# The first layer's input projection in another order, with new on-chip places for its branch

## The chip, the cores and the metric

One core of a Trainium2 chip runs the whole program. The metric is the device time of one execution in microseconds (us). Five engines work beside each other, each through its own queue in order: TensorE (PE, with its weight loads PEld), VectorE (DVE), ScalarE (ACT), GpSimd (POOL) and SyncE (SP), which here issues the DMA transfers.

## The reference

Two layers of a diffusion backbone on 1152 columns of width 1024: 1024 latent tokens (conditioned by `c`) and 128 context tokens (conditioned by `c_ctx`). Layer 0 mixes with a bidirectional recurrence and a pooling branch, layer 1 with attention; each has a squared-ReLU MLP behind. What the change touches is the mixer of layer 0:

```python
hp = modulate(x, p['g_mix'], shift, scale)          # rms_norm(x)*(1+scale)+shift
z = h @ p['w_in']                                   # 1024 -> 1536
xr, gate, xpool = jnp.split(z, [D_RNN, 2 * D_RNN], axis=-1)   # 512 each
xc = dwconv_centred(xr, p['conv_w'], p['conv_b'])   # 4 taps along the sequence
r = sigmoid(xc @ w_a + b_a); i = sigmoid(xc @ w_i + b_i)      # both directions
a = exp(8 r log_sigmoid(lam)); u = sqrt(1 - a*a) * (i * xc)
h_t = a_t h_{t-1} + u_t                             # forward and backward scan
y_rnn = (hf + hb) * gelu(gate)
y_pool = ((window mean - xpool) @ w_pool) * s_pool  # windows 2, 4, 8, 16
out = concat([y_rnn, y_pool]) @ p['w_out']
```

The states of the recurrence at the ends of the context are an output too.

## The kernel before

Features lie on the 128 partitions, the sequence along the row. `w_in` is cut into 12 units of 128 output features: 0 to 3 recurrent channels, 4 to 7 gate channels, 8 to 11 pooling groups with windows 2, 4, 8 and 16. The sequence is cut into three chunks of 384 columns (chunk 2 holds 256 latent and 128 context columns). `project(u, hs, c)` computes one unit for one chunk in one PSUM bank: 24 matmuls, since every fp32 operand is split into a high and a low fp32r part and three of their products are summed (`mm3`, lines 166 to 168; `split`, lines 162 and 163: ACT copies the high part, DVE or POOL subtracts for the low part). There are 8 banks.

In the beginning `mod_steps` (line 200) multiplies the conditioning by `w_mod`, for shift and scale of the first norm. `first_norm` squares a chunk (ACT), sums the squares (DVE and POOL by turns), gets the root through two small matmuls (`Norm.stat`, lines 280 and 289) and multiplies (line 383); `modulate` with `inplace` scales and shifts (line 304) and splits. `first_units` then projects units 11, 10 and 9 (u3) as chunks become ready. Units 8, 0, 1, ..., 7 follow in the loop over `order`; behind each chunk stands `hook(w, c)`, which carries the other work of the branch:

- `windows(g, pb)`: the doubling sums of a pooling group (line 556, POOL and DVE by turns), its edges (POOL), the difference (line 563), its split into `xh` and `xl`; in a second step the 9 pooling matmuls, and the store of the result to device memory (lines 573 and 574).
- `conv(m, xr)` (lines 484 and 487, DVE), `gates(m, xc)` (split of `xc` into the same single pair `xh`, `xl`; 36 matmuls; 12 sigmoids, line 507) and `lru(m, xc, z)` (lines 518 to 539: tanh, exp, square root on ACT, products on DVE and POOL, four scans on DVE, the sum of both directions). The four gate results and four temporaries come from a ring of 10 buffers.
- `mod_bg(2)` behind chunks 1 and 2: two steps each of `mod_steps` for the later modulations, each step one weight load and two matmuls, each ninth step a transpose (line 207).

Gates and recurrences stand at units 2 to 5. The GELU and the last product (`rnn_out`, lines 544 and 546) wait until the last square root was issued. Then `out_proj` (first matmul: `ps_b<-mix_yh`) reads the pooled channels back from device memory.

PE's order is the program's; a scheduler sets the others, but for SP's transfers of the beginning. Behind the beginning all loads of weights and for `mod_steps` share three `w_raw` buffers.

Of the kernel before, what the change touches and what calls it, by code (L numbers as in the profile page):

```python
# [77 lines left out]
def emit(tc, A, O):  # L78
# [216 lines left out]
    def modulate(norm, x, c, hs, l, ffn, lo_eng=(po, ve), inplace=False, spare=None):  # L295
# [3 lines left out]
        for k in range(KT):  # L299
            xn = x[c][:, k, :]  # L300
            sh = lambda g: mod[l][:, sh0 + k, g:g + 1]
            if inplace:
                for a, b, g in groups(c, norm.ch):
                    ve.tensor_scalar(xn[:, a:b], xn[:, a:b], scl[:, k, g:g + 1], sh(g), op0=OP.mult, op1=OP.add)
                split(hh[:, k, :], hl[:, k, :], xn, eng=lo_eng[k % len(lo_eng)])
                continue
# [145 lines left out]
    pbs = {}  # L452
    for g in (3, 2, 1):
        pbs[g] = gslot()
        pads(pbs[g], 8)
# [54 lines left out]

    hst = {}

    def lru(m, xc, z):
# [75 lines left out]
    pw = parts(load(A["w_pool"], 512), sl, "wg", 1)  # L589
    wnd = {g: windows(g, pbs[g]) for g in (3, 2, 1)}  # L590
    next(wnd[3])
    ys, xr, xcs, gl_ = {}, {}, {}, {}

    def gate_products(m):
        return lru(m, xcs[m], next(gl_[m]))

    def hook(w, c):

        nonlocal last
# [2 lines left out]
        if w == 8 and c == 2:
            wnd[0] = windows(0, pbs[0])
        at = {(8, 1): 3, (0, 0): 2, (0, 2): 1, (1, 1): 0}.get((w, c))
        if at is not None:
            next(wnd[at])
            if at:
                next(wnd[at - 1])
# [976 lines left out]
```

## Time and profile before

| | us |
|---|---|
| median of 3 runs (lowest, highest) | 2928.2 (2923.76, 2932.3) |
| the profiled execution | 2933.02 |
| its span | 2931.0 |
| PE, DVE, ACT, POOL busy in the span | 2781.7, 1896.3, 1354.9, 1155.2 |

The profile is of one execution, and its times count from the start of its span. A row of the windows shows: from and to, length, busy time of PE, PEld, DVE, ACT and POOL (with counts), PE's granted clock as a share of 2.4 GHz, the DMA engines' busy share, and GB/s. A timeline row shows start and duration of instructions of one line; the time in brackets is how long the engine sat idle before and what released it. Ends of matmuls are modelled, so their starts are read.

### The profile page before, as it was taken

Reading aid. Unit: us, or ns where it says so; the run is one execution under the profiler, and the core shown is the slowest. Engines: PE = TensorE matmul, PEld = TensorE weight load, DVE = VectorE, ACT = ScalarE, POOL = GpSimd, SP = SyncE. Lnnn points to the kernel's source line nnn. Section 1 sums busy time; section 2 is a strip of 40 time slices with the busy share of each in tenths; the row PEclk is TensorE's granted clock in tenths of the full one; section 3 lists DMA queues with packets and bytes.
Section 4 is the critical chain, followed back from the end, with each engine's and each line's share of the span. In section 5 each row is a group of like instructions: output and inputs, shape, how many; then the busy total and the mean of one; then the engine's idle time right before and its main releaser. Section 6 shows DMA issues by size and latency. Waiting matters only on the chain.

```text
span 2931.0 us, 51557 instructions
## 1 busy us (share of the span) xinstructions
PE 2781.7 (95%) x19896; PEld 2685.8 (92%) x19896; DVE 1896.3 (65%) x3534; ACT 1354.9 (46%) x3143; POOL 1155.2 (39%) x968
## 2 busy tenths in 40 slices
PE   5897799999999999898999999998999999999997
PEld 3886698999999999898999999988999999999997
DVE  5559677666555788965777777776841112368887
ACT  3356343222335233455777777774432223433335
POOL 3434111112138878313323233321111112688853
PEclk8999899999999999999999999999999999999998
DMA  5233514666564554420000000024244444455452
GB/s 228 87 124 97 182 44 160 211 211 206 207 224 164 197 188 157 148 70 21 21 14 22 13 15 23 23 63 134 77 169 158 164 153 158 156 194 194 157 163 89
DMA packets 144941, 372.78 MB, mean 127 GB/s; under 512 B 15944, under 2 KB 49080, under 8 KB 143288
## 3 DMA queue, kind: packets, MB, share of 16 engines
q1 hardware_dynamic: 144696, 369.50, 37.2%
q8 instruction: 156, 2.56, 0.4%
q14 instruction: 89, 0.73, 0.1%
HBM read 260.68 MB, written 108.75 MB: 126 GB/s over the span
## 4 chain that ended last, share of the span: by engine, by line
PE 77%; DVE 12%; ACT 4%; issue 3%; DMA 2%; POOL 2%; SPq 0%; DVEq 0%; ACTq 0%; POOLq 0%
PE ps_b L166 19%; PE ps_b L167 19%; PE ps_b L168 19%; PE pS_t L1129 3%; PE pS_o L1147 3%; PE pS_s L166 3%; PE pS_s L168 2%; PE pS_s L167 2%; ACT aw_p L1122 1%; PE pS_g L166 1%; PE pS_g L168 1%; PE pS_g L167 1%; DVE x_t L352 1%; DVE acc_t L827 1%; ACT aw_ph L1133 1%
## 5 line engine op out<-in xcount | busy, mean ns | idle before, releaser
L765 POOL TENSOR_TENSOR fu_r<-fu_r 128x576 f32<-128x576 f32 x128 | 160.4, 1253 | 669.9 <-ACT fu_ah L764 640.7
L167 PE MATMUL ps_b<-ht_t,wl_hlh 128*128 128x288 f32 (+1 forms) x1312 | 404.4, 308 | 13.8 <-DVE ht_t L163 9.2
L166 PE MATMUL ps_b<-ht_t,wl_hlh 128*128 128x288 f32 (+1 forms) x1312 | 407.4, 311 | 6.4 <-ACT ht_t L162 5.0
L168 PE MATMUL ps_b<-ht_t,wl_hll 128*128 128x288 f32 (+1 forms) x1312 | 402.0, 306 | 0.0
L766 DVE TENSOR_TENSOR fu_ah<-fu_r,fu_ah 128x576 fp32r<-128x576 f32 (+1 forms) x128 | 89.1, 696 | 356.1 <-POOL fu_r L765 356.1
L759 ACT ACTIVATE fu_r<-ps_b 128x288 f32<-128x288 f32 x256 | 104.2, 407 | 432.8 <-PE ps_b L168 427.1
L882 DVE TENSOR_TENSOR acc_t<-ps_b,acc_t 128x288 f32<-128x288 f32 x656 | 269.8, 448 | 51.0 <-PE ps_b L168 49.3
L166 PEld LDWEIGHTS ps_b<-ht_t,wl_hlh 128*128 128x128 f32 x1312 | 249.6, 190 | 21.1 <-issue 6.7
L167 PEld LDWEIGHTS ps_b<-ht_t,wl_hlh 128*128 128x128 f32 x1312 | 250.3, 191 | 17.0 <-DVE ht_t L163 10.5
L162 ACT ACTIVATE wl_hlh<-w_raw 128x1024 fp32r<-128x1024 f32 (+1 forms) x161 | 137.7, 863 | 268.4 <-PE ps_b L167 205.0
L1137 DVE TENSOR_TENSOR aw_pl<-pS_t,aw_ph 128x384 fp32r<-128x384 f32 (+1 forms) x400 | 200.5, 541 | 84.7 <-ACT aw_ph L1133 79.1
L168 PEld LDWEIGHTS ps_b<-ht_t,wl_hll 128*128 128x128 f32 x1312 | 250.7, 191 | 0.0
L166 PE MATMUL ps_b<-fq_at,wl_hlh 128*128 128x288 f32 x800 | 238.0, 298 | 1.6 <-DVE acc_t L882 1.1
L168 PE MATMUL ps_b<-fq_at,wl_hll 128*128 128x288 f32 x800 | 235.4, 294 | 0.0
L167 PE MATMUL ps_b<-fq_at,wl_hlh 128*128 128x288 f32 x800 | 234.8, 293 | 0.0
L1122 ACT ACTIVATE aw_p<-pS_s,aw_nb 128x384 f32<-128x384 f32 (+1 forms) x400 | 225.1, 580 | 17.9 <-DVE aw_nb L1116 17.0
L1112 DVE TENSOR_REDUCE aw_mx<-pS_s 128x1 f32<-128x384 f32 (+1 forms) x400 | 203.7, 539 | 34.9 <-PE pS_s L168 33.8
L1133 ACT ACTIVATE aw_ph<-pS_t 128x384 fp32r<-128x384 f32 (+1 forms) x400 | 174.1, 487 | 86.4 <-PE pS_t L1129 85.7
L163 DVE TENSOR_TENSOR wl_hll<-w_raw,wl_hlh 128x1024 fp32r<-128x1024 f32 (+1 forms) x109 | 139.4, 1279 | 99.9 <-ACT wl_hlh L162 98.7
L696 POOL TENSOR_TENSOR fb_b<-fb_b 128x576 f32<-128x576 f32 x112 | 176.6, 1588 | 25.5 <-DMA fb_b<-dram_t 21.6
L166 PE MATMUL ps_b<-fq_at,fw_hlh 128*128 128x288 f32 x576 | 172.0, 299 | 4.6 <-DVE acc_t L882 3.3
L167 PE MATMUL ps_b<-fq_at,fw_hlh 128*128 128x288 f32 x576 | 170.0, 295 | 0.0
(394 smaller groups left out, 8902.1 us busy)
## 6 DMA issues: line engine op xcount, KB each, us to landing
fq_at<-dram_t SPq DMA_DIRECT2D x76, 576.0 KB, 3.9
dram_t<-fu_ah SPq DMA_DIRECT2D x72, 576.0 KB, 2.9
w_raw<-in_ffn SPq DMA_DIRECT2D x64, 512.0 KB, 3.8
dram_t<-fu_r SPq DMA_DIRECT2D x112, 288.0 KB, 2.1
fb_b<-dram_t SPq DMA_DIRECT2D x28, 1152.0 KB
fq_at<-in_w_mod SPq DMA_DIRECT2D x128, 192.0 KB, 4.1
w_raw<-in_l_ffn_w SPq DMA_DIRECT2D x40, 512.0 KB, 4.8
w_raw<-in_w_mod SPq DMA_DIRECT2D x32, 512.0 KB, 4.2
```

The source lines that it names most:

```text
L162: act(hi, src, AF.Copy)
L163: eng.tensor_tensor(lo, src, hi.bitcast(F32), op=OP.subtract)
L166: mm(out, wh, hh, start=start, stop=False)
L167: mm(out, wh, hl, start=False, stop=False)
L168: mm(out, wl, hh, start=False, stop=stop)
L696: po.tensor_tensor(a[:, :, o, :], a[:, :, p, :], a[:, :, q, :], op=op)
L765: po.tensor_tensor(r, r, r, op=OP.mult)
L882: ve.tensor_tensor(to, b, to, op=OP.add)
L1112: ve.tensor_reduce(self.mx[:, i:i + 1], self.sc[i][0], axis=AX.X, op=OP.max)
L1122: act(self.pt[i][:, :w], v, AF.Exp, bias=self.nb, accum_out=lsum[:, self.h, self.blk, i:i + 1])
L1133: act(hi[g][:, :self.nks[g], j * P:(j + 1) * P], self.tp[g], AF.Copy)
L1137: ve.tensor_tensor(lo[g][s_], self.tp[g], hi[g][s_].bitcast(F32), op=OP.subtract)
```

## The change

Units 0, 1 and 2 are projected at first, then 3, 11, 10, 4, 9, 5, 8, 6 and 7. Each recurrence starts as soon as its channels are there; pooling groups and gate channels lie between. GELU and last product stand behind the third chunk of each gate unit. The result of a recurrence is written over its input slot `xr[m]`. The ring has 8 buffers, convolution slots are 3, three `p` slots hold pooling and gate channels, and the pooling weights are loaded group by group. `mod_bg` gets one step behind chunks 0 and 1, two behind chunk 2. The first norm now multiplies scale and root in one pass, the shift is added by ACT (high part) and DVE (low part), as the later norms do it. All splits of `xh` and `xl` and all window sums go to DVE.

```diff
 def first_norm(c):
-            nm.square(c, xin[c][:, k, :], eng=(ve, po)[k % 2])
+            nm.square(c, xin[c][:, k, :], eng=ve)
         yield from nm.stat(c)
-            ve.tensor_tensor(xin[c][:, k, :], xin[c][:, k, :], nm.rs[c], op=OP.mult)
+                ve.scalar_tensor_tensor(xv[:, a:b], xv[:, a:b], sc_mix[0][:, k, g:g + 1], nm.rs[c][:, a:b],
+                                        op0=OP.mult, op1=OP.mult)
+    def shifted(c):
...
+                act(hs[c][0][:, k, a:b], xv[:, a:b], AF.Identity, bias=sh)
+                ve.scalar_tensor_tensor(hs[c][1][:, k, a:b], xv[:, a:b], sh, hs[c][0][:, k, a:b].bitcast(F32),
+                                        op0=OP.add, op1=OP.subtract)
...
-    first_units((1, 2), (1, 1), (2, 3), (2, 2), (2, 1))
+    first_units((1, 1), (1, 2), (2, 0))
-    ring = lambda: sr.t([P, RW], tag="r", bufs=10)[:, :TL]
-    cslot = lambda: sl.t([P, PADW], tag="c", bufs=4)
+    ring = lambda: sr.t([P, TL], tag="r", bufs=8)
+    cslot = lambda: sl.t([P, PADW], tag="c", bufs=3)
+    pslot = lambda: sl.t([P, PADW], tag="p", bufs=3)
 def gates / windows
-        split(xh, xl, xc, eng=po)
+        split(xh, xl, xc)
-            (po, ve)[i % 2].tensor_tensor(nx[:, :n], cur[:, :n], cur[:, k:k + n], op=OP.add)
+            ve.tensor_tensor(nx[:, :n], cur[:, :n], cur[:, k:k + n], op=OP.add)
-        split(dh, dl, d, eng=po)
+        split(dh, dl, d)
+        pw = parts(load(A["w_pool"][:, g * P:(g + 1) * P], P), sl, "pw", 1)
...
+    def recurrence(m):
+        z = next(gl_[m])
+        if m in (1, 2):
+            next(wnd[4 - m])
+        lru(m, xcs[m], z)
+        if m < 3:
+            xcs[m + 1] = conv(m + 1, xr[m + 1])
+
+    HOOKS = {(3, 0): [(recurrence, 0), (before_gates, 1)], (10, 0): [(recurrence, 1)],
+             (4, 0): [(next, 3), (before_gates, 2)], (9, 0): [(recurrence, 2)],
+             (5, 0): [(next, 2), (before_gates, 3)], (8, 0): [(recurrence, 3), (next, 1)],
+             (6, 0): [(next, 1), (next, 0)], (7, 0): [(next, 0)]}
 def hook(w, c):
-        if c:
-            mod_bg(2)
...
+        mod_bg(1 + (c == 2))
+        for f, i in HOOKS.get((w, c), ()):
+            f(wnd[i] if f is next else i)
+    xcs[0] = conv(0, xr[0])
+    before_gates(0)
+    first_units((2, 1), (2, 2))
-    order = (8, 0, 1, 2, 3, 4, 5, 6, 7)
+    order = (3, 11, 10, 4, 9, 5, 8, 6, 7)
...
+        if 3 < w < 8:
+            rnn_out(w - 4, dst)
-    with tc.issue_after(last.ins if hasattr(last, "ins") else last):
-        for m in range(4):
-            rnn_out(m, ys[m])
```

Order on DVE in the first norm of chunk 0, before (`n_t` is the chunk, `n_rs` its root, `ht_t_102` and `ht_t_103` its high and low parts, `n_acc` sums of squares, `wl` split weights):

```order
L383 TENSOR_TENSOR n_t_114<-n_t_114,n_rs_273 128x384 x8
L211 TENSOR_TENSOR const_t_93<-ps_b_309,const_t_77 128x16
L212 TENSOR_TENSOR const_t_93<-ps_b_309,const_t_93 128x16
L304 TENSOR_SCALAR n_t_114<-n_t_114,const_t_95,const_t_93 128x384 x8
L270 TENSOR_TENSOR n_acc_353<-n_acc_353,n_sq_358 128x384
L163 TENSOR_TENSOR wl_hll_295<-w_raw_292,wl_hlh_294 128x1024
L163 TENSOR_TENSOR ht_t_103<-n_t_114,ht_t_102 128x384 x2
L163 TENSOR_TENSOR wl_hll_301<-w_raw_298,wl_hlh_300 128x1024
L163 TENSOR_TENSOR ht_t_103<-n_t_114,ht_t_102 128x384 x2
```

and now:

```order
L379 SCALAR_TENSOR_TENSOR n_t_114<-n_t_114,const_t_95,n_rs_273 128x384 x8
L210 TENSOR_TENSOR const_t_93<-ps_b_309,const_t_77 128x16
L211 TENSOR_TENSOR const_t_93<-ps_b_309,const_t_93 128x16
L269 TENSOR_TENSOR n_acc_345<-n_acc_345,n_sq_347 128x384
L269 TENSOR_TENSOR n_acc_345<-n_acc_345,n_sq_350 128x384
L389 SCALAR_TENSOR_TENSOR ht_t_103<-n_t_114,const_t_93,ht_t_102 128x384 x8
L162 TENSOR_TENSOR wl_hll_295<-w_raw_292,wl_hlh_294 128x1024
```

Two whole passes over the chunk with the splits behind have become one pass and the low parts; the sums of the next chunk are no longer shared with POOL.

Order on DVE in the first recurrence before, from line 530 to the first scans (`ring_r` are gates and temporaries, `slots_c` convolutions, `slots_wg` gate weights):

```order
L530 SCALAR_TENSOR_TENSOR ring_r_1400<-ring_r_1400,ring_r_1336 128x1160
L484 TENSOR_SCALAR slots_c_1554<-gslot_g_1448,const_t_77 128x1160
L530 SCALAR_TENSOR_TENSOR ring_r_1401<-ring_r_1401,ring_r_1368 128x1160
L531 TENSOR_TENSOR ring_r_1352<-ring_r_1400,ring_r_1352 128x1160
L487 SCALAR_TENSOR_TENSOR slots_c_1554<-gslot_g_1448,const_t_77,slots_c_1554 128x1160
L163 TENSOR_TENSOR wl_hll_1668<-w_raw_1665,wl_hlh_1667 128x1024
L531 TENSOR_TENSOR ring_r_1384<-ring_r_1401,ring_r_1384 128x1160
L535 SCALAR_TENSOR_TENSOR ring_r_1336<-ring_r_1402,const_t_77,ring_r_1352 128x1024
L535 SCALAR_TENSOR_TENSOR ring_r_1336<-ring_r_1402,ring_r_1352 128x128
```

and in the second recurrence now (`slots_p` are pooling channels, `slots_x` the split inputs of the gates and pooling matmuls):

```order
L559 TENSOR_TENSOR slots_c_1555<-slots_p_1090 128x1175
L535 SCALAR_TENSOR_TENSOR ring_r_1214<-ring_r_1214,ring_r_1129 128x1160
L162 TENSOR_TENSOR slots_wgl_1380<-w_raw_1377,slots_wgh_1379 128x512
L535 SCALAR_TENSOR_TENSOR ring_r_1215<-ring_r_1215,ring_r_1161 128x1160
L559 TENSOR_TENSOR slots_c_1556<-slots_c_1555 128x1173
L536 TENSOR_TENSOR ring_r_1145<-ring_r_1214,ring_r_1145 128x1160
L162 TENSOR_TENSOR slots_xl_1374<-slots_c_1246,slots_xh_1373 128x1160
L536 TENSOR_TENSOR ring_r_1177<-ring_r_1215,ring_r_1177 128x1160
L559 TENSOR_TENSOR slots_c_1555<-slots_c_1556 128x1169
L540 SCALAR_TENSOR_TENSOR ring_r_1129<-ring_r_1216,const_t_77,ring_r_1145 128x1024
L540 SCALAR_TENSOR_TENSOR ring_r_1129<-ring_r_1216,ring_r_1145 128x128
L540 SCALAR_TENSOR_TENSOR ring_r_1161<-ring_r_1217,const_t_77,ring_r_1177 128x1024
```

Between the recurrence's own products there now stand the window sums of a pooling group and the split for the next gates; before there were a convolution's taps.

Order on SP at the end of the branch, before (`const_t_119` holds the end states, `dram_t` the pooled channels, the other loads are weights):

```order
L172 DMA w_raw_2254<-in_w_mod 128x1024
L172 DMA w_raw_2285<-in_w_mod 128x1024
L924 DMA out_lru<-const_t_119 128x8
L911 DMA nt_xn_2397<-dram_t_753 128x288
L172 DMA w_raw_2385<-in_l_w_out 128x1024
```

and now:

```order
L171 DMA w_raw_2226<-in_w_mod 128x1024
L171 DMA w_raw_2273<-in_w_mod 128x1024
L926 DMA out_lru<-const_t_119 128x8
L171 DMA w_raw_2304<-in_w_mod 128x1024
L577 DMA dram_t_691<-slots_p_1823 128x1024
L578 DMA dram_t_691<-slots_p_1823 128x128
L913 DMA nt_xn_2407<-dram_t_691 128x288
L171 DMA w_raw_2395<-in_l_w_out 128x1024
L171 DMA w_raw_2399<-in_l_w_out 128x1024
```

The store of the end states no longer stands directly ahead of the loads for the output projection; the last pooling group's store does.

## Rows read from the trace of the kernel before

**Rows 1.** Windows of four stretches, columns as said in the profile section.

```profile
41.00:102.90 61.90, 48.30 (x243) 45.92 (x244) 43.88 (x78) 26.56 (x56) 29.43 (x21) 0.83 0.12 34
102.90:315.20 212.30, 182.25 (x971) 154.21 (x970) 152.79 (x112) 114.17 (x164) 94.55 (x69) 0.94 0.35 112
315.20:325.10 9.90, 0.04 (x1) 0.05 (x1) 5.88 (x11) 1.71 (x3) 0.00 (x0) 0.62 0.48 154
325.10:443.10 118.00, 111.11 (x805) 109.00 (x806) 79.08 (x177) 42.65 (x95) 17.68 (x18) 0.96 0.31 110
```

**Rows 2.** The waits of PE from 41 to 103 us: total, times, longest.

```profile
PE ps_b L167 <- DVE ht_t L163: 9.2, 3, 4.0
PE ps_b L166 <- ACT ht_t L162: 5.0, 2, 4.3
PE ps_b L280 <- POOL n_acc L270: 2.3, 1, 2.3
```

**Rows 3.** The waits of PE from 103 to 315.2 us, all of them.

```profile
PE ps_b L200 <- DMA w_raw<-in_w_mod: 9.3, 5, 3.9
PE ps_b L207 <- ACT w_raw L204: 7.6, 3, 4.9
PE ps_b L166 <- ACT ring_r L507: 5.3, 3, 2.2
PE ps_b L167 <- POOL slots_xl L163: 4.6, 1, 4.6
PE ps_b L166 <- ACT slots_xh L162: 1.7, 1, 1.7
PE ps_b L200 <- DVE ps_b L195: 1.1, 1, 1.1
PE ps_b L166 <- ACT gslot_g L445: 0.5, 1, 0.5
```

**Rows 4.** Timeline of PE: start, duration, line, tiles, [idle before <- releaser].

```profile
55.91 0.42 PE L166 MATMUL ps_b<-ht_t,wl_hlh 128*128 128x384 f32 x1
...
60.00 0.34 PE L168 MATMUL ps_b<-ht_t,wl_hll 128*128 128x384 f32 x1
...
142.85 1.04 PE L200 MATMUL ps_b<-w_raw,const_t 128*2 128x512 f32 x8
...
299.84 1.03 PE L200 MATMUL ps_b<-w_raw,const_t 128*2 128x512 f32 x4
...
314.51 0.66 PE L207 MATMUL ps_b<-const_t,w_raw 128*128 128x128 f32 x4 [0.70 <-ACT w_raw L204]
325.06 0.61 PE L166 MATMUL ps_b<-mix_yh,wl_hlh 128*128 128x288 f32 x1 [9.88 <-ACT mix_yh L162]
```

**Rows 5.** Timeline of ACT, same columns.

```profile
61.04 0.49 ACT L291 ACTIVATE n_rs<-ps_b 128x384 f32<-128x384 f32 x1
...
102.75 0.39 ACT L443 ACTIVATE gslot_g<-ps_b 128x256 f32<-128x256 f32 x1 [2.83 <-PE ps_b L168]
...
271.19 2.96 ACT L507 ACTIVATE ring_r<-ps_b,const_t 128x384 f32<-128x384 f32 x6
```

**Rows 6.** Timeline of DVE.

```profile
34.91 4.64 DVE L383 TENSOR_TENSOR n_t<-n_t,n_rs 128x384 f32<-128x384 f32 x8 [4.36 <-ACT n_rs L291]
...
242.95 3.86 DVE L531 TENSOR_TENSOR ring_r<-ring_r,ring_r 128x1160 f32<-128x1160 f32 x1
...
318.80 0.28 DVE L539 TENSOR_TENSOR slots_c<-ring_r,ring_r 128x128 f32<-128x128 f32 x1
```

**Rows 7.** Timeline of POOL.

```profile
242.52 3.07 POOL L526 TENSOR_TENSOR ring_r<-ring_r,slots_c 128x1160 f32<-128x1160 f32 x1 [0.70 <-ACT ring_r L507]
```

**Rows 8.** DVE groups by form, 400 to 480 us: busy, mean ns.

```profile
L314 DVE SCALAR_TENSOR_TENSOR ht0a_t<-nt_xn,const_t,ht0a_t 128x288 fp32r<-128x288 f32 x16 | 8.0, 512 | 0.0
```

**Rows 9.** DVE groups by form, 95 to 325 us.

```profile
L524 DVE SCALAR_TENSOR_TENSOR ring_r<-ring_r,ring_r 128x1160 f32<-128x1160 f32 x8 | 10.6, 1353 | 0.0
```

**Rows 10.** Timeline of the SP queue.

```profile
318.91 0.34 SPq L924 DMA_DIRECT2D out_lru<-const_t  x1
```

More of the change, by code (lines that the diff above doesn't have):

```diff
@@ L33 @@
 LCH = [(0, 384), (384, 384), (768, 392)]
-PADW = TL + 24
-RW = TL + 8
+PADW = TL + 16
 NK = T + NP
@@ L293, in stat, with modulate @@
                 then(c)
-    def modulate(norm, x, c, hs, l, ffn, lo_eng=(po, ve), inplace=False, spare=None):
+    def modulate(norm, x, c, hs, l, ffn, spare):
         scl = (sc_ffn if ffn else sc_mix)[l]
@@ L301, in modulate @@
             sh = lambda g: mod[l][:, sh0 + k, g:g + 1]
[L302 to L306, printed above, removed]
             xs = spare.t([P, norm.ch], tag="xn", bufs=2)
@@ L389, in emit @@
     lst = cs.t([P, 8])
-    tl = cs.t([P, 4, 8])
-    l0, l1, l2, l3 = (tl[:, j, :] for j in range(4))
     def decay():
@@ L417, in emit @@
     st = Scope("start", side="right")
+    tl = st.t([P, 4, 8])
+    l0, l1, l2, l3 = (tl[:, j, :] for j in range(4))
     decay()
@@ L432, in emit @@
         nc.sync.dma_start(xin[1], A["x"][1])
-        u3[2] = w0(10)
-        u3[1] = w0(9)
+        u3[1] = w0(1)
+        u3[2] = w0(2)
         nc.sync.dma_start(xin[2], A["x"][2])
@@ L450, in pads @@
         po.memset(t[:, p0 + TL:PADW], 0.0)
[L452 to L455, printed above, removed]
+    xr = {}
+    for m in range(3):
+        xr[m] = gslot()
+        pads(xr[m], 2)
     n1, n2 = first_norm(1), first_norm(2)
@@ L527, in lru @@
         for d in range(2):
-            last = act(S[d], S[d], AF.Sqrt)
+            act(S[d], S[d], AF.Sqrt)
         for d in range(2):
@@ L538, in lru @@
         for a, e in ((0, NS), (POFF, TL)):
-            ve.tensor_tensor(xc[:, a:e], R[0][:, a:e], R[1][:, a:e], op=OP.add)
-        hst[m] = xc
-        return last
+            ve.tensor_tensor(xr[m][:, a:e], R[0][:, a:e], R[1][:, a:e], op=OP.add)
     def rnn_out(m, y):
@@ L588, in emit, with before_gates @@
     pd = dr.t([4, P, T])
[L589 to L595, printed above, removed]
-    def hook(w, c):
-        nonlocal last
-        if c:
-            mod_bg(2)
[L602 to L608, printed above, removed]
-        if w < 4 and c == 2:
-            xcs[w] = conv(w, xr[w])
-        g = {(2, 0): (None, 0), (2, 2): (0, 1), (3, 2): (1, 2), (4, 2): (2, 3), (5, 2): (3, None)}.get((w, c))
-        if g:
-            if g[0] is not None:
-                last = gate_products(g[0])
-            if g[1] is not None:
-                gl_[g[1]] = gates(g[1], xcs[g[1]])
-                next(gl_[g[1]])
-    last = None
-    order = (8, 0, 1, 2, 3, 4, 5, 6, 7)
+    xcs, gl_, wnd = {}, {}, {}
+    def before_gates(m):
+        gl_[m] = gates(m, xcs[m])
+        next(gl_[m])
+    def recurrence(m):
[9 more added lines that the diff above has]
+             (6, 0): [(next, 1), (next, 0)], (7, 0): [(next, 0)]}
+    def hook(w, c):
+        mod_bg(1 + (c == 2))
[5 more added lines that the diff above has]
+    order = (3, 11, 10, 4, 9, 5, 8, 6, 7)
     for i, w in enumerate(order):
@@ L625, in emit @@
             us0 = [unit(A["l0_w_out"][k * P:(k + 1) * P, :]) for k in (4, 5)]
-        if w == 8:
-            dst, off = pbs.setdefault(0, gslot()), 8
-        elif w < 4:
+        if w == 3:
             dst, off = xr.setdefault(w, gslot()), 2
+        elif w > 7:
+            dst, off = pslot(), 8
+            wnd[w - 8] = windows(w - 8, dst)
         else:
-            dst, off = ys.setdefault(w - 4, gslot()), 0
+            dst, off = (cslot if w == 5 else pslot)(), 0
         if off:
```

42 lines of the change are left out of this document (24 added, 18 removed).

## The prediction

> **What bounds the kernel now.** I read the table of windows first, then the waits of PE, then its timeline, and last the engines that PE waits for. The windows cut out the part that the change can reach: the first projection begins near 41 us, the ninth unit-chunk is evacuated at 102.75 [rows 5], the last matmul of the branch stands at 314.5 and the output projection begins at 325.06 [rows 4]. Behind that all five engines carry the same instructions in the same order but for a few neighbours, so I look only at this part. PE shows busy for 182 of 212 us in the long stretch [rows 1], which hides how far it is from its own work. That work is counted from rows: 23 matmul steps from 55.91 to 60.00 give 0.178 us each [rows 4], so a chunk of 24 takes 4.27.
>
> From 102.9 to 315.2 us stand 27 chunks (115.3 us), 144 gate matmuls (25.6), 36 pooling matmuls (6.4), 18 slots of `mod` matmuls at 1.04 (18.7) and four transposes at 0.66 (2.6): 168.6 us. The stretch takes 212.3. Of the 43.7 us above, 30.1 are waits that the view of waits names in sum [rows 3]. I take the other 13.6 for matmuls at the lower clock level: the granted clock there is 0.94 of 2.4 GHz in the mean, of stretches at 2.4 and at 1.2 [rows 1]. So 1 us of wait has cost 1.45 us in all; I use this ratio below. The waits are scattered: `mod` loads, the copy ahead of a transpose, sigmoids that wait for ring buffers, a POOL split. In front (41 to 102.9) PE waits mostly for the high and low parts of a chunk [rows 2]; at the end it waits 9.88 us once [rows 4].
>
> **The first norm.** Removed are one DVE pass over each chunk and POOL's share of the sums and low parts; added are DVE passes for all sums and all low parts. A pass of 384 columns takes 4.64/8 = 0.58 us [rows 6]; the same kind of instruction as the new ones takes 0.512 at 288 columns [rows 8]. I take 0.6 for the new ones. Chunk 0: the root is there at 34.91 [rows 6], eight products end at 39.7, two sums of the next chunk 40.8, eight low parts 45.6. Five more sums and two weight splits bring the next statistic to about 51; with the two small matmuls and their copies chunk 1's root is there at 56.5 instead of 61.04 [rows 5]. Sixteen passes later, 66.1, its low parts are complete, and its third statistic's root follows at 68.5. Chunk 2 is cut in two groups, 32 instructions of about 0.45 (estimated between those rows for 256 and 128 columns): 83. PE projects two chunks beside that, ends the seventh at 84 and the ninth at 92.5, against 102.75: a gain of 10. If the passes take 0.68 (0.512 scaled by columns) and the clock stays low between short waits, 3 are left; if PE only misses the first chunk's waits again, 15.
>
> **The `mod` steps.** Pairs and single steps take the same time: 1.04 for eight records, 1.03 for four [rows 4]. One, one and two steps behind three chunks make three slots of two; counted through, 25 slots with matmuls stand where 18 stood. That costs 7 x 1.04 = 7.3. In return the transposes no longer follow directly on their copy: a chunk stands between, but for the last. This takes most of the 7.6 us of that wait [rows 3].
>
> **The recurrences.** They are moved forward, and their latency is to lie beside the other units. From gates to gates PE has now 36 gate matmuls (6.4), six chunks (25.6), mostly 9 pooling matmuls (1.6) and five or six slots (5.2 to 6.2): 37.9, 39.8 and 39.5 us for the three spacings. The chain from the first sigmoid to the last sum took 271.19 to 319.08, 47.9 us, the one time that nothing but the end stood behind it [rows 5, 6]. With 8 ring buffers the next gates need what this chain releases, so up to 8 to 10 us are missing each time. But buffers come free one by one: half of them before the scans end. I expect one spacing to miss its 8 us (the second, where ACT's copy for a transpose stands ahead of the sigmoids and waits for a weight split that DVE does behind the scans), the other two nearly none. I add 2 for `mod` loads that find `w_raw` held by weights not yet split, and 3 for the last load and transpose. That is 13 us of waits, 18.9 with the ratio, against 43.7: a gain of 24.8. Bounds: 43.7 if no wait is left; with all three spacings missing (26.5) and the 5, 31.5 x 1.45 = 45.7, a loss of 2.
>
> What else DVE takes over (eight splits of 1160 columns, six window sums, at 1.353 each [rows 9], 18.9 us) I cost at nothing: DVE is busy for 152.8 of 212.3 us in the stretch [rows 1], and the splits are ready before PE asks for them, as the chunks between leave over 15 us. If that cover is gone, it is the rival with the long chain below. The two extra table loads on ACT are hidden too (busy 114 of 212 [rows 1]). The additional small pooling loads go behind one another on SP and lie three chunks ahead of their use.
>
> **The end.** Before, SP's store of the end states went out at 318.91 [rows 10], right behind the last sum, and the loads for the output projection stood behind it. Now the last recurrence ends some 8 chunks earlier; what PE waits for is ACT: copy, GELU, a weight split and the first high part, some 4 us. Gain 6, bounds 0 and 9.9.
>
> **The sum.** 10 - 7.3 + 24.8 + 6 = 33.5. It is made against the profiled execution, 2933.0, which is 4.8 above the median of 2928.2. So 2899.5 there, and 2895 against the median. With all bounds at once the gain lies between -6 and 61.
>
> **POOL in DVE's way.** At 242.95 a DVE product took 3.86 us beside a POOL product that lasted from 242.52 to 245.59 [rows 6, 7]; alone such an instruction takes 1.353 [rows 9]. It ended 1.22 behind POOL's end, so it stood still. The Trainium skill (SBUF — State Buffer, section "SBUF: two separate sides") states that a DVE instruction with two SBUF inputs and a GpSimd instruction that reads SBUF hold a port pair by turns, for a whole instruction. By that rule the trace's 3.86 is explained, and the change cuts both ways: POOL loses its splits and sums, but each recurrence keeps POOL's two products of 3.07, and DVE has more to do beside them.
>
> **Rivals.**
> 1. POOL's two products hold DVE in each chain for their whole length: 6.1 us more in each of three spacings, 18.4, all paid by PE. Waits are 31.4 instead of 13, 45.5 with the ratio, and the gain shrinks to 6.8: 2921. For it speaks the row of 3.86; against it that only two of the recurrence's DVE instructions can meet them in the worst place.
> 2. No waits are left behind the ninth unit-chunk and the first norm gains its 15: 61, so 2867. Against it: 8 buffers in place of 10.
> 3. Slower: DVE's queue makes one chain of everything. Window sums, difference and split (up to 6 x 1.353 = 8.1), convolution (5.4) and the next split (1.4) stand between the products and lengthen the 47.9 us to nearly 63, and the next gates wait for its end. Three spacings then miss 70 us; with the 5 that is 108.7 instead of 43.7, and the time is 2984. It turns into a loss when a chain with all that lasts over some 49.5 us from gates to gates. For it speaks that these instructions do stand between the recurrence's own in DVE's order; against it that in the 47.9 us DVE itself waited for buffers and POOL, time that the added work fills.
> 4. The gain is given back: the recurrences are early, but pooling and gate channels, stores and loads set the same end. Within 9 us of 2928.
>
> **How the numbers follow.** Forecast (a gain of 20 to 48, 2880 to 2908): 0.60. Rival 2: 0.08. Rival 1: 0.18, half of it faster. Rival 3: 0.08. Rival 4: 0.06. About 0.3% (9 us) can be told from no change. So faster 0.60 + 0.08 + 0.09 + 0.01 = 0.78, same 0.14, slower 0.08. The range reaches from most of rival 2 to rival 1: 2874 to 2922.
>
> **What would show it.** Right: the ninth unit-chunk is evacuated near 92 us; the output projection begins near 290; PE's waits between are near 13 us, the largest at the third unit's gates with ACT as releaser; the wait ahead of the output projection is below 5. Wrong: PE waits for `slots_xl` or `ring_r` by 8 us or more at each gate or pooling group (rival 3), DVE products of 3 us and more in every recurrence (rival 1), or differences behind the start of the output projection, which I hold to be none.

## The result, and the profile after

| | before | changed |
|---|---|---|
| median of the runs, us (lowest, highest) | 2927.61 (2923.76, 2932.3) | 2875.65 (2870.8, 2877.94) |
| profiled execution, its span | 2933.02, 2931.0 | 2875.85, 2874.1 |
| ninth unit-chunk evacuated | 102.75 | 86.36 |
| first matmul of the output projection | 325.06 | 272.94 |
| first matmul of the MLP | 443.1 | 392.2 |

The changed kernel takes 0.982 of the time, with a 95% interval of 0.980 to 0.984: 52 us less. The forecast was 2895, 32.6 less than the median of before. The sign held; 2875.65 lies below the main band of the forecast (2880 to 2908) and 1.7 us inside its stated range (2874 to 2922), so the gain was sized too small and the range held narrowly. The two places divide it: 16.4 us lie ahead of the ninth unit-chunk and 35.7 between it and the output projection. I call the time between these two the stretch: 222.3 us before (325.06 less 102.75), 186.6 now. Behind it the profiled pair differs by another 5 us; the judgement below shows that this is not the change.

The windows of the changed kernel, at the places that answer to the first three of [rows 1]:

```profile
37.70:86.50 48.80, 45.08 (x242) 43.64 (x243) 41.78 (x88) 29.11 (x64) 0.21 (x4) 0.92 0.16 55
86.50:271.30 184.80, 177.78 (x971) 146.78 (x970) 157.67 (x130) 116.26 (x169) 60.73 (x49) 1.00 0.42 135
271.30:272.90 1.60, 0.00 (x0) 0.00 (x0) 1.56 (x4) 1.59 (x3) 0.00 (x0) 1.00 0.88 324
```

The second row holds the same 971 matmuls on record in 184.8 us instead of 212.3. POOL fell from 94.55 to 60.73 us, DVE rose by only 4.9 although 18.9 us of work were moved to it (two taps of a convolution, 2.9 us, now lie ahead of the window), and the granted clock rose from 0.94 to 1.00 of 2.4 GHz.

The waits of PE, first from 37.7 to 86.5 us, which answer to [rows 2], then from 86.5 to 271.3, which answer to [rows 3] (total, times, longest):

```profile
PE ps_b L165 <- ACT ht_t L388: 3.3, 1, 3.3
PE ps_b L279 <- DVE n_acc L269: 2.9, 1, 2.9
...
PE ps_b L199 <- DMA w_raw<-in_w_mod: 2.5, 3, 1.3
PE ps_b L199 <- DVE ps_b L194: 2.2, 3, 1.0
PE ps_b L165 <- ACT ring_r L514: 1.1, 1, 1.1
PE ps_b L206 <- ACT w_raw L203: 0.7, 1, 0.7
PE ps_b L165 <- ACT w_raw L203: 0.4, 1, 0.4
```

In the long stretch 30.1 us of waits became 6.9, and no single one lasts over 1.3. The wait for POOL's `slots_xl` is gone, the one for the copy ahead of a transpose is nearly gone.

The timeline of PE at the end, against [rows 4]:

```profile
270.61 0.66 PE L206 MATMUL ps_b<-const_t,w_raw 128*128 128x128 f32 x4 [0.70 <-ACT w_raw L203]
272.94 0.40 PE L165 MATMUL ps_b<-mix_yh,wl_hlh 128*128 128x288 f32 x1 [1.68 <-ACT mix_yh L161]
```

The 9.88 us ahead of the output projection are 1.68. Then ACT's roots and the ninth evacuation, against [rows 5]:

```profile
55.00 0.49 ACT L290 ACTIVATE n_rs<-ps_b 128x384 f32<-128x384 f32 x1 [0.18 <-PE ps_b L288]
65.52 0.49 ACT L290 ACTIVATE n_rs<-ps_b 128x384 f32<-128x384 f32 x1 [0.18 <-PE ps_b L288]
86.36 0.39 ACT L449 ACTIVATE gslot_g<-ps_b 128x256 f32<-128x256 f32 x1 [2.84 <-PE ps_b L167]
```

And DVE's passes of the first norm, against the first row of [rows 6]:

```profile
32.39 4.32 DVE L379 SCALAR_TENSOR_TENSOR n_t<-n_t,const_t,n_rs 128x384 f32<-128x384 f32 x8 [4.34 <-ACT n_rs L290]
...
71.32 5.35 DVE L389 SCALAR_TENSOR_TENSOR ht_t<-n_t,const_t,ht_t 128x256 fp32r<-128x256 f32 x16
```

Eight passes of chunk 0 take 4.32 us, 0.54 each. The 16 low parts of chunk 2 (eight of 256 and eight of 128 columns) take 5.35, 0.33 each, and are complete at 76.67.

### The profile page after: what moved, and what is told of

Same layout as the page of the kernel before. It is cut to its first block, busy times and chain, and to the rows that moved or that the text cites. A ratio compares the mean times of both kernels' runs of the same rounds, so it can differ in the third digit from the quotient of the medians.

```text
span 2874.1 us, 51555 instructions
## 1 busy us (share of the span) xinstructions
PE 2771.8 (96%) x19896; PEld 2673.2 (93%) x19896; DVE 1901.5 (66%) x3559; ACT 1357.3 (47%) x3156; POOL 1083.3 (38%) x930
## 4 chain that ended last, share of the span: by engine, by line
PE 77%; DVE 12%; ACT 4%; issue 3%; DMA 2%; POOL 1%; SPq 0%; DVEq 0%; ACTq 0%; POOLq 0%
PE ps_b L165 20%; PE ps_b L166 19%; PE ps_b L167 19%; PE pS_o L1149 3%; PE pS_t L1131 3%; PE pS_s L165 3%; PE pS_s L167 2%; PE pS_s L166 2%; ACT aw_p L1124 1%; PE pS_g L165 1%; PE pS_g L167 1%; DVE x_t L346 1%; PE pS_g L166 1%; DVE acc_t L829 1%; ACT aw_ph L1135 1%
## 5 line engine op out<-in xcount | busy, mean ns | idle before, releaser
L1124 ACT ACTIVATE aw_p<-pS_s,aw_nb 128x384 f32<-128x384 f32 (+1 forms) x400 | 224.7, 578 | 15.6 <-DVE aw_nb L1118 14.7
L1114 DVE TENSOR_REDUCE aw_mx<-pS_s 128x1 f32<-128x384 f32 (+1 forms) x400 | 203.1, 538 | 31.2 <-PE pS_s L167 30.1
L1135 ACT ACTIVATE aw_ph<-pS_t 128x384 fp32r<-128x384 f32 (+1 forms) x400 | 173.6, 486 | 82.0 <-PE pS_t L1131 81.6
L162 DVE TENSOR_TENSOR wl_hll<-w_raw,wl_hlh 128x1024 fp32r<-128x1024 f32 (+1 forms) x109 | 129.9, 1192 | 85.0 <-ACT wl_hlh L161 84.1
```

The source lines that it names most:

```text
L162: eng.tensor_tensor(lo, src, hi.bitcast(F32), op=OP.subtract)
L1114: ve.tensor_reduce(self.mx[:, i:i + 1], self.sc[i][0], axis=AX.X, op=OP.max)
L1124: act(self.pt[i][:, :w], v, AF.Exp, bias=self.nb, accum_out=lsum[:, self.h, self.blk, i:i + 1])
L1135: act(hi[g][:, :self.nks[g], j * P:(j + 1) * P], self.tp[g], AF.Copy)
```

## Experiments

Three batches of four kernels, each batch on one chip beside the kernel before (medians 2929.8, 2929.39 and 2929.3 us). Each profile is of one execution. The ninth unit-chunk lies up to 5 us apart in runs with the same first norm (100.4 to 105.6 with the old one, 83.2 to 88.0 with the new), so I read from the profiles the stretch, from the ninth unit-chunk to the output projection. It repeats to 0.4 us (186.6, 186.9 and, with the old norm, 186.9):

| run | median, us | ratio to before (95%) | ninth chunk | stretch | waits in it | clock in it |
|---|---|---|---|---|---|---|
| before | 2929.4 | 1 | 102.75 | 222.3 | 40.0 | 0.92 |
| changed, again | 2878.75 | 0.9825 (0.9805 to 0.9845) | 87.05 | 186.9 | 8.7 | 1.00 |
| norm alone | 2913.4 | 0.994 (0.9927 to 0.9954) | 88.01 | 222.2 | 39.1 | 0.91 |
| order alone | 2895.6 | 0.9878 (0.9865 to 0.9892) | 102.43 | 186.9 | 8.3 | 0.99 |
| store late | 2922.17 | 0.9975 (0.9965 to 0.9984) | 105.45 | 214.7 | 34.0 | 0.95 |
| POOL shares | 2890.74 | 0.9868 (0.9854 to 0.9881) | 87.14 | 197.5 | 15.7 | 0.97 |
| mod pairs | 2876.69 | 0.9818 (0.98 to 0.9837) | 83.16 | 190.5 | 15.2 | 0.96 |
| mod layout | 2874.49 | 0.9816 (0.9798 to 0.9835) | 84.68 | 188.7 | 14.6 | 0.96 |
| ring of 7 | 2879.51 | 0.983 (0.9811 to 0.9849) | 87.44 | 190.9 | 10.7 | 0.98 |
| before, mod singles | 2932.85 | 1.0013 (1.0004 to 1.0022) | 105.63 | 221.2 | 31.7 | 0.91 |
| before, DVE for POOL | 2916.21 | 0.9953 (0.994 to 0.9966) | 100.4 | 208.4 | 30.7 | 0.93 |
| ACT scalars | 2868.94 | 0.979 (0.9772 to 0.9807) | 85.59 | 179.2 | 4.1 | 1.00 |
| ACT scalars and layout | 2859.63 | 0.9757 (0.9741 to 0.9772) | 85.89 | 173.6 | 5.0 | 1.00 |

**The norm alone, in the kernel before**

```diff
-            nm.square(c, xin[c][:, k, :], eng=(ve, po)[k % 2])
+            nm.square(c, xin[c][:, k, :], eng=ve)
...
-    modulate(nm, xin, 0, hs, 0, False, inplace=True)
+    shifted(0)
...
```

> The kernel before with only the new first norm (one pass of scale and root, shift in the splits, all sums on DVE); order of units, ring and recurrences as before. Theory (the gains add up by place): the ninth unit-chunk is evacuated some 13 to 16 us earlier than 102.75 and all behind it moves up by that, so 2912 (2909 to 2916) against 2927.6. Rival (the stretch behind is held by its own loads and recurrences, and gives it back): PE's waits between 90 and 315 us grow by 8 or more, 2920 or above. The term of the prediction, 10 us, would be 2917.6.

Measured: 16.4 us less, the ninth unit-chunk 14.7 earlier than in the profile of before, and a stretch of 222.2 against 222.3. The theory holds: what the norm gains in front is kept to the last. The forecast's 10 falls.

**The order alone, with the norm of before**

```diff
...
-    shifted(0)
+    modulate(nm, xin, 0, hs, 0, False, inplace=True)
...
```

So this run has all of the change but the norm: the order, the ring, the `mod` steps and DVE's new work.

> The changed kernel with the first norm of before (root in one pass, scale and shift in a second, splits and sums shared with POOL); everything else new. Theory (the gains add up by place): it keeps the 36 us that the long stretch and the end gave, 2892 (2887 to 2896); its ninth unit-chunk is evacuated 13 to 16 us later than 86.36, and PE's waits behind it stay near 7 us. Rival (the new order lives on the early start, since DVE is nearly full in the recurrences): a later first recurrence meets the gates, PE waits for ring_r or slots_xl by 5 us or more, and the time is 2900 or above.

Measured: 34.2 us less. The ninth unit-chunk is as late as before (102.43) and the stretch as short as in the changed kernel (186.9). Both runs together give 16.4 + 34.2 = 50.6 of the 51 to 52, so the two halves add up and do not depend on each other.

**The end-state store behind the loads, in the kernel before**

```diff
...
-        elif c == 0:
-            nc.sync.dma_start(O["lru"], lst)
...
+            if c == 3:
+                with tc.issue_after(xload.ins if hasattr(xload, "ins") else xload):
+                    nc.sync.dma_start(O["lru"], lst)
```

> The kernel before with one transfer moved: the store of the end states stands behind the loads of x instead of ahead of the first load for the output projection. Theory (that store, which waits for the last sum, holds SP's queue and so the loads): the wait of 9.88 us falls to about 2, and the time to 2919.5 (2917 to 2922). Rival (PE waits for ACT and the pooled channels anyway): the wait stays above 7 us and the time within 3 us of 2927.6.

SP's queue of that run at the end of the branch (start, duration, line, transfer):

```profile
310.11 0.42 SPq L911 DMA_DIRECT2D nt_xn<-dram_t  x1
310.62 4.47 SPq L172 DMA_DIRECT2D w_raw<-in_l_w_out  x2
...
325.58 0.34 SPq L925 DMA_DIRECT2D out_lru<-const_t  x1
```

The loads for the output projection go out at 310 instead of 319, the store at 325.58. PE's wait falls from 9.88 to 4.03, where the theory had about 2, and the time by 7.6 us, where it had 8.1. So the store did hold the queue; 4 us are left, and they end with ACT.

**POOL shares the splits and sums again, in the changed kernel**

```diff
-        split(xh, xl, xc)
+        split(xh, xl, xc, eng=po)
...
-            ve.tensor_tensor(nx[:, :n], cur[:, :n], cur[:, k:k + n], op=OP.add)
+            (po, ve)[i % 2].tensor_tensor(nx[:, :n], cur[:, :n], cur[:, k:k + n], op=OP.add)
...
-        split(dh, dl, d)
+        split(dh, dl, d, eng=po)
```

> The changed kernel with the low parts of xh and xl subtracted on POOL again and the window sums by turns on POOL and DVE. Theory A (DVE has room, POOL's instructions stand in its way and are slower): PE waits for slots_xl at two or more pooling groups or gates, 5 us in sum, 2881 (2877 to 2886). Theory B (the chunks between cover either engine): within 3 us of 2875.7. Theory C (DVE is the tight engine here, 9 to 10 tenths busy from 105 to 255 us): the relief shortens the recurrences by 5 us each, PE waits 3 us less, 2872.

Measured: 12.0 us above the repeat of the changed kernel (which ran on another chip), more than each theory gave. The stretch is 10.6 longer. PE does not wait for `slots_xl` at all, so theory A has the sign and not the place. Its longest wait is one of these three:

```profile
PE ps_b L199 <- DMA w_raw<-in_w_mod: 6.8, 3, 4.3
```

It can be followed back. Four engines of this run in order of time:

```profile
137.41 3.85 DVE L559 TENSOR_TENSOR slots_c<-slots_c 128x1161 f32<-128x1161 f32 x1 [1.96 <-POOL slots_c L559]
...
147.57 9.19 DVE L494 SCALAR_TENSOR_TENSOR slots_c<-gslot_g,const_t,slots_c 128x1160 f32<-128x1160 f32 x3
...
148.52 3.80 POOL L162 TENSOR_TENSOR slots_xl<-slots_c,slots_xh 128x1160 fp32r<-128x1160 f32 x1
152.27 3.27 POOL L559 TENSOR_TENSOR slots_c<-slots_p 128x1175 f32<-128x1175 f32 x1
...
159.24 1.21 DVE L162 TENSOR_TENSOR wl_hll<-w_raw,wl_hlh 128x1024 fp32r<-128x1024 f32 x1
...
160.48 4.44 SPq L171 DMA_DIRECT2D w_raw<-in_w_mod  x3
...
164.53 1.87 PE L199 MATMUL ps_b<-w_raw,const_t 128*2 128x512 f32 x4 [4.29 <-DMA w_raw<-in_w_mod]
```

And the same in the changed kernel:

```profile
142.75 5.91 DVE L494 SCALAR_TENSOR_TENSOR slots_c<-gslot_g,const_t,slots_c 128x1160 f32<-128x1160 f32 x3
...
153.69 1.22 DVE L162 TENSOR_TENSOR wl_hll<-w_raw,wl_hlh 128x1024 fp32r<-128x1024 f32 x1
...
154.93 1.18 SPq L171 DMA_DIRECT2D w_raw<-in_w_mod  x2
```

Three taps of a convolution take 9.19 us beside POOL's split and sum; in the changed kernel the same three took 5.91. They also begin 4.8 us later (0.8 of it because the ninth unit-chunk is later in this run): ahead of them DVE idles 1.96 us for a window sum of POOL's, and its own next sum takes 3.85 us. The weight split queued behind them comes at 159.24 instead of 153.69. The next load takes the buffer that this split gives back: the split ends at 160.45 and the `mod` loads go out at 160.48, where the changed kernel has 154.91 and 154.93, and PE stands 4.29 us. Here POOL's work reaches PE by way of DVE's queue and a shared load buffer, not by the tile that POOL writes. The other waits of this run were not followed back.

**The changed kernel again, with mod pairs, and with a ring of 7**

> The changed kernel once more, as the measure for the three beside it. All theories: 0.982 of the kernel before, 2877 (2873 to 2881) where that takes 2929.8; the output projection begins within 2 us of 272.9.

```diff
-        mod_bg(1 + (c == 2))
+        if c:
+            mod_bg(2)
```

> The changed kernel with the mod steps in pairs again, two behind chunks 1 and 2 and none behind chunk 0. Theory (a pair costs what a single step costs, the prediction's term of 7.3): 18 slots instead of 25, 7 us less work for PE, given back in part since transposes stand right behind their copy again (about 1 us each, 2 to 3 in sum): 4 to 5 us less than the changed kernel, 2872. Rival (two loads at a time into three shared buffers come late): PE waits for w_raw by 7 us or more, as in the kernel before, and the time is that of the changed kernel or up to 8 above it.

```diff
+    steps = iter([2, 0, 2, 2, 0, 2, 1] * 3 + [2, 2, 2, 0, 2, 1])
...
-        mod_bg(1 + (c == 2))
+        mod_bg(next(steps, 2))
```

> The changed kernel with the mod steps in pairs laid out so that a transpose never follows its copy directly (2, 0, 2, 2, 0, 2, 1 steps behind seven chunks, and so on): 16 slots with matmuls instead of 25. Theory: 9 x 1.04 = 9.4 us less work for PE, 2868 (2865 to 2872), waits for w_raw and its transposes below 5 us. Rival (three shared buffers): waits for w_raw of 7 us or more take most of it, 2874 to 2880.

```diff
-    ring = lambda: sr.t([P, TL], tag="r", bufs=8)
+    ring = lambda: sr.t([P, TL], tag="r", bufs=7)
```

> The changed kernel with 7 ring buffers instead of 8. Theory (buffers come free one by one long before the chain ends, and the next gates meet free ones): PE's waits for ring_r grow by less than 3 us at each gate unit, 2880 (2876 to 2887). Rival (8 is the edge, the missing 8 us of the prediction lie right behind it): PE waits for ring_r by 5 us or more at three gate units, and with the slow clock behind each wait the time is 2900 or above.

The repeat agrees with the first: 2878.75, and the output projection begins at 273.91. PE's waits with pairs, and then with the layout:

```profile
PE ps_b L199 <- DVE ps_b L194: 7.2, 2, 5.5
PE ps_b L206 <- ACT w_raw L203: 4.9, 2, 4.2
...
PE ps_b L199 <- DMA w_raw<-in_w_mod: 1.2, 2, 0.7
```

```profile
PE ps_b L199 <- DMA w_raw<-in_w_mod: 11.9, 7, 5.0
```

Pairs save seven slots of 1.04 us and the layout nine, yet the stretches are 3.6 and 1.9 us longer than in the repeat. The waits are of 4 to 5.5 us again, for a bank that DVE has to clear, for the copy and for loads, and the clock is 0.96 instead of 1.00. The ratios are within the interval of the changed kernel. The layout's rival holds in full. Of the pairs' rival only the time holds: loads cost PE 1.2 us there and not 7, the bank 7.2 and the copy 4.9. With the layout the way from the output projection to the MLP takes 114.4 us, where the repeat takes 119.8; this 5.4 is part of its time, and its cause was not tried.

With 7 ring buffers the wait for `ring_r` stays at 1.1 us and the ratio within the interval, so 8 was not the edge that the rival meant. The stretch is 4.0 us longer all the same, with 2.0 us more of other waits and a clock of 0.98.

**Two parts of the change in the kernel before**

```diff
-        if c:
-            mod_bg(2)
+        mod_bg(1 + (c == 2))
```

> The kernel before with one edit: mod steps one, one and two behind the three chunks of a unit instead of two behind chunks 1 and 2. From the ninth unit-chunk to the output projection before takes 222.3 us. Theory (single steps bring 7.3 us more matmul time and take the copy's 7.6 us of waits away): 222, the time within 4 us of 2929.5. Rival (pairs cost less, nothing comes back): 230, 2937. Rival (pairs were the worse choice there too, as in the run with pairs in the new order, whose stretch was 4 us longer): 216 to 218, 2924.

Measured: 3.6 us slower by the medians, the interval just off 1, and a stretch 1.1 shorter. This looks even, as the theory had it, but a second thing changed with the edit: the scheduler put the store of the end states at 337.01, behind the loads for the output projection, which begin at 310.23. In the run with the store late this alone shortened the stretch by 7.6. Beside that run the stretch here is 6.5 longer: the matmul time grows by 7.3 (by the count of slots), the copy's waits fall from 7.4 to 3.4, and the waits for `ring_r` grow from 3.5 to 9.8. So, if the store is worth as much here, the single steps cost about the prediction's 7.3 in the order of before, and the theory's even balance is not shown. More is lost behind the stretch: from the output projection to the MLP it takes 122.2 us (326.8 to 449.0) where before took 118.0; PE's waits for `mix_yl` there are 10.3 instead of 6.9 and the granted clock 0.94 instead of 0.96. Why was not tried.

```diff
-        split(xh, xl, xc, eng=po)
+        split(xh, xl, xc)
...
-            (po, ve)[i % 2].tensor_tensor(nx[:, :n], cur[:, :n], cur[:, k:k + n], op=OP.add)
+            ve.tensor_tensor(nx[:, :n], cur[:, :n], cur[:, k:k + n], op=OP.add)
...
-        split(dh, dl, d, eng=po)
+        split(dh, dl, d)
```

> The kernel before with one edit: all splits of xh and xl and all window sums on DVE. Theory (POOL's work beside DVE's products costs in either order): the wait for slots_xl (4.6 us) goes, DVE's products get shorter, the stretch of 222.3 us falls by 8 or more, 2919 (2914 to 2922). Rival (it pays only where recurrences and pooling run beside each other): the stretch stays within 4 us, 2926 to 2933.

PE's waits in that stretch, and SP's queue at its end:

```profile
PE ps_b L200 <- DMA w_raw<-in_w_mod: 16.7, 3, 11.7
...
PE ps_b L166 <- ACT mix_yh L162: 2.3, 1, 2.3
PE ps_b L166 <- ACT ring_r L507: 2.0, 2, 1.6
```

```profile
293.36 0.42 SPq L911 DMA_DIRECT2D nt_xn<-dram_t  x1
298.22 7.23 SPq L172 DMA_DIRECT2D w_raw<-in_l_w_out  x2
...
321.91 0.34 SPq L924 DMA_DIRECT2D out_lru<-const_t  x1
```

Measured: 13.1 us less, the stretch 13.9 shorter. The sign is the theory's: more work on DVE makes the kernel faster in the old order too, and DVE is busy 161.8 us in the stretch where it was 158.6. The size is not shown, because here too the scheduler put the store of the end states behind the loads for the output projection. If the store is worth as much here as in the run that moved it alone, some 6 us of the time and of the stretch are left, so DVE's part lies somewhere from 6 to 13. The waits for `slots_xl`, `slots_xh` and most of `ring_r` are gone, and the wait at the end is 2.3 instead of 9.88 us. This old order then pays 16.7 us for `mod` loads, 11.7 of them at once, which the new one does not.

**POOL's scalar passes on ACT, without and with the layout**

```diff
-            po.tensor_scalar(R[d], R[d], 1.0, 1.0, op0=OP.mult, op1=OP.add)
+            act(R[d], R[d], AF.Identity, bias=ones[:, 0:1])
...
-            po.tensor_scalar(Q[d], R[d], -0.5, -1.0, op0=OP.mult, op1=OP.add)
+            act(Q[d], R[d], AF.Copy, bias=-1.0, scale=-0.5)
```

> The changed kernel with the four scalar passes of each recurrence on POOL (lines 527 and 530) moved to ACT. Theory (POOL's work still holds DVE): the convolution's taps and the products of lines 528 and 535 fall from 1.7 to 2.2 us to below 1.5, DVE is less busy in the stretch by 8 us or more, and PE's waits fall from 7 us to 4: 2875 (2871 to 2878). Rival (ACT holds evacuations behind passes that wait for DVE): PE's waits on ACT or on banks grow by 5 us or more, 2883 or above.

> The changed kernel with the scalar passes on ACT and the mod steps in the layout 2, 0, 2, 2, 0, 2, 1. Theory (w_raw buffers were late because DVE's weight splits stood behind slowed products): PE's waits for w_raw fall from the 11.9 us of that layout alone to 6 or less, the stretch takes 180 us (before 222.3, changed 186.6), 2869 (2865 to 2873). Rival (three buffers don't carry two loads at a time, whatever DVE does): waits for w_raw of 10 us or more, 2874 or above.

DVE's groups by form in the stretch (busy, mean ns, idle before): the changed kernel, then with POOL sharing, then with the scalar passes on ACT.

```profile
L494 DVE SCALAR_TENSOR_TENSOR slots_c<-gslot_g,const_t,slots_c 128x1160 f32<-128x1160 f32 x10 | 20.5, 2054 | 0.3
L535 DVE SCALAR_TENSOR_TENSOR ring_r<-ring_r,ring_r 128x1160 f32<-128x1160 f32 x8 | 13.5, 1712 | 0.0
L528 DVE SCALAR_TENSOR_TENSOR ring_r<-ring_r,ring_r 128x1160 f32<-128x1160 f32 x8 | 13.4, 1708 | 2.1 <-POOL ring_r L527 2.1
```

```profile
L535 DVE SCALAR_TENSOR_TENSOR ring_r<-ring_r,ring_r 128x1160 f32<-128x1160 f32 x8 | 20.4, 2576 | 0.0
L528 DVE SCALAR_TENSOR_TENSOR ring_r<-ring_r,ring_r 128x1160 f32<-128x1160 f32 x8 | 12.6, 1598 | 0.0
```

```profile
L494 DVE SCALAR_TENSOR_TENSOR slots_c<-gslot_g,const_t,slots_c 128x1160 f32<-128x1160 f32 x10 | 18.3, 1836 | 0.2
L535 DVE SCALAR_TENSOR_TENSOR ring_r<-ring_r,ring_r 128x1160 f32<-128x1160 f32 x8 | 10.7, 1358 | 0.0
```

The very same product of line 535 costs 2.58, 1.71 and 1.36 us, as POOL has 103.7, 60.7 and 32.8 us to do in the stretch. Not every product follows POOL's sum: line 528 takes 1.60 with POOL sharing and 1.71 without, so it matters which of POOL's instructions lies beside it. DVE as a whole is busy 144.6 us instead of 159.4, with the same 135 instructions. Against the theory the taps of line 494 stay at 1.84: POOL's product of line 531 is left beside them, and the longest tap, of 3.72 us, ends 1.2 behind such a product. The gain over the repeat of the changed kernel is 9.8 us where 3 to 4 were expected (the two intervals overlap at their ends), and the stretch is 7.6 shorter. The theory was right in kind, and the rival (ACT in the way) did not come, although ACT's busy time in the stretch rose from 118.0 to 135.5 us.

With the layout on top, the windows row of the stretch and its waits:

```profile
85.90:259.50 173.60, 168.56 (x973) 146.98 (x971) 146.27 (x136) 135.74 (x189) 35.23 (x34) 1.00 0.46 152
```

```profile
PE ps_b L165 <- ACT mix_yh L161: 3.1, 1, 3.1
PE ps_b L199 <- DMA w_raw<-in_w_mod: 1.9, 2, 1.0
```

The layout alone waited 11.9 us for `w_raw`; with DVE free of POOL's scalar passes it waits 1.9. The same three buffers now carry two loads at a time, so the rival falls. At 2859.63 us this version beats both kernels; its interval, 0.9741 to 0.9772, lies below that of the changed kernel. Of its 19.1 us below the repeat the stretch has 13.3, and 5.4 lie between the output projection and the MLP, as with the layout alone.

## Why the prediction was right, and where its sizes failed

**First norm: forecast 10, measured 16.4.** The mechanism was right, the size was off, and past its upper bound of 15. By the forecast chunk 1's root came at 56.5, chunk 2's at 68.5, its low parts at 83 and the ninth chunk at 92.5; measured were 55.00, 65.52, 76.67 and 86.36. The size is not the scatter of one pair of profiles: the run with the norm alone gives 16.4 by its medians, and the ninth unit-chunk stands at 103.3 in the mean of five profiles with the old norm and at 86.1 in nine with the new. A pass took 0.54 us, not 0.6, and the 32 instructions of chunk 2 10.7, not the 14.4 that 0.45 each makes. Left out was that POOL's share of the sums leaves the first statistic too. POOL's group of additions in the kernel before, up to 60 us, and the first statistic on PE, with the `mod` steps ahead of it, in the kernel before and in the changed one:

```profile
L270 POOL TENSOR_TENSOR n_acc<-n_acc,n_sq 128x384 f32<-128x384 f32 x11 | 13.2, 1206 | 36.8 <-ACT n_sq L269 28.9 <-DVE n_acc L270 7.1 <-ACT const_col L282 0.7
```

```profile
22.37 3.06 PE L200 MATMUL ps_b<-start_raw,const_t 128*2 128x512 f32 x8 [3.93 <-DVE n_acc L270]
27.81 1.44 PE L280 MATMUL ps_b<-const_t,n_acc 128*128 128x1 f32 x6 [2.38 <-POOL n_acc L270]
```

```profile
21.20 3.07 PE L199 MATMUL ps_b<-start_raw,const_t 128*2 128x512 f32 x8 [3.92 <-DMA start_raw<-in_w_mod]
25.29 1.44 PE L279 MATMUL ps_b<-const_t,n_acc 128*128 128x1 f32 x6 [1.03 <-DVE n_acc L269]
```

An addition takes 1.206 us on POOL, twice a DVE pass. The statistic starts 2.5 us earlier now, but only 1.35 of it is POOL's share: behind the start of those `mod` steps it comes after 5.44 us with the old norm and after 4.09 with the new, in every run to 0.03. The other 1.2 us lie ahead of them, and there the runs with either norm overlap.

**`mod` steps: forecast a loss of 7.3.** The added work is there (25 slots where 18 stood), but in the new order it costs nothing as a choice: put back to pairs, the changed kernel is no faster and its stretch longer by 3.6. In the forecast's accounts the payment is in the next term, where the transposes' wait goes. In the order of before the single steps do cost, 6.5 us beside the run with the store late.

**Recurrences: forecast 24.8, measured 34.8.** With 175.9 us of PE's own work, as the forecast counted it (168.6 + 7.3), the 184.8 us to the last transpose leave 8.9 above, where before 43.7 stood. Two sizes were off. Waits were 6.9 instead of 13: the expected 8 us at the third unit's gates came at that place and with that releaser, and were 1.1 and 0.4. And the ratio of 1.45 stood for matmuls at the lower clock level, where the granted clock is 1.00 now; 8.9 / 6.9 is 1.29. Of the 10 us by which the term was too small, the waits make 8.8 and the ratio 1.1, which is less than the count of PE's own work is good for (some 2 us, by the last section).

The step that failed is the sentence that DVE's additional work costs nothing. It is a gain: 12.0 us by the run that took it out of the changed kernel, and somewhere from 6 to 13 in the kernel before. With POOL sharing again, the new order shows 14.0 us of waits up to its last transpose and 19.7 us above PE's own work, against the forecast's 13 and 18.9. So the forecast's sum fits the kernel without this step. Its places do not, as the wait for `ring_r` is 1.1 there too, so that this agreement is in part luck. Rival 1 had named the lock and priced it as a loss that the change would meet; the change removed a large part of it. Its sign is there in part: four DVE instructions of the stretch take 3.7 to 3.9 us, two taps and two pooling differences, but no product of a recurrence does, and PE's 6.9 us of waits show that it did not pay for them. The Trainium skill's rule in the prediction (SBUF — State Buffer, section "SBUF: two separate sides") agrees with the three durations of line 535 above; what it led to was misjudged, since I counted POOL's two products and not its splits and scalar passes.

**The end: forecast 6, measured 8.3** (9.88 to 1.68 us of wait). Moving the store alone gave 7.6 in time with a wait of 4.03, so the named cause is shown. That the rest came from the earlier GELU and last product was not tried apart. Whether DVE's work shortens this wait by itself stays open: the run that has it in the old order (2.3) has the store late as well.

**The sum.** 16.4 - 7.3 + 34.8 + 8.3 = 52.2 at the start of the output projection, against 33.5. Rival 2 (no waits left, 2867) was nearer in kind than its 0.08; rival 3 (one long DVE chain) did not come, though DVE is busy for 157.67 of 184.8 us; rival 4 is excluded by the additive halves. Of the 34.2 us of the order alone 12.0 are DVE's additional work, by the run with POOL sharing; how the other 22 divide between the moved recurrences, the store, the ring and the `mod` steps was not tried in the new order.

**Behind the start of the output projection: forecast none.** The gain is 52.1 there, 50.9 at the MLP and 56.9 at the span's end. The 6 us come up in the attention: from the first matmul on `hin_t` to the first of `ht2a_h` with MLP weights it takes 862.3 us before and 856.5 after, but 862.0 in the repeat of the changed kernel. So it belongs to the execution and not to the change.

## What to carry to other kernels

Work that POOL does beside a busy DVE is not free help: before giving it a share, look at what the DVE instructions beside it take, and try the share on DVE or ACT even where DVE looks full. Follow a late load back to who gives its buffer back; here a POOL instruction delayed a weight split, the split a buffer, the buffer a load, and the load PE. A count of fewer instructions (pairs for single steps) gains only once the buffers behind it come free in time. And compare the order of the DMA queue in every run: edits of one or three lines to DVE's and PE's work moved a store here that is worth 7.6 us by itself.

## What the runs showed of the hardware that was not expected

The prediction counted only POOL's two-input products as being in DVE's way. Its scalar passes with one input held DVE back too: with them on ACT, line 535's product fell from 1.71 to 1.36 us. The changed kernel's timeline shows it instruction by instruction:

```profile
157.22 2.23 POOL L530 TENSOR_SCALAR ring_r<-ring_r 128x1160 f32<-128x1160 f32 x1 [1.29 <-DVE ring_r L529]
158.35 2.31 DVE L535 SCALAR_TENSOR_TENSOR ring_r<-ring_r,ring_r 128x1160 f32<-128x1160 f32 x1
161.18 1.35 DVE L535 SCALAR_TENSOR_TENSOR ring_r<-ring_r,ring_r 128x1160 f32<-128x1160 f32 x1
```

The first product ends at 160.66, 1.21 us behind POOL's scalar pass, as the prediction's product of 3.86 ended 1.22 behind POOL's. The second has no POOL instruction beside it and takes 1.35.

What the waits cost beyond themselves follows no fixed ratio. I take PE's own work by the forecast's count (175.9 us, with pairs 168.6, with the layout 166.5) and the waits from the stretch. With 4.1 us of waits (scalar passes on ACT) -0.8 us are left, with 5.0 (the same and the layout) 2.1, with 8.6 (changed) 2.1, with 10.7 (ring of 7) 4.2, with 15.2 (pairs) 6.7, with 14.6 (layout) 7.6, and with 40.0 (before) 13.7. The granted clock is 1.00 in the first three, then 0.98, 0.96, 0.96 and 0.92. As -0.8 and 2.1 at the same clock show, the count of own work is uncertain by some 2 us. The longest wait does not order these runs: with the ring of 7 none is over 1.7, and 4.2 are left. So no rule from the length of a wait is shown, and no exact ratio for the changed kernel.
